# A two-layer decoder trunk on one core: the MLP groups' two matmuls with the high weights joined into one of 512 columns

## Chip, cores and metric

The kernel runs on one core of one Trainium2 chip. The metric is the device time of one execution in microseconds, as a median over runs. TensorE (PE) multiplies, VectorE (DVE) and ScalarE (ACT) do the elementwise work, and SyncE (SP) issues the large loads.

## What is computed

One sequence of 256 tokens of width 2048 passes through two layers. Layer 0 mixes tokens with a sparse attention (NSA), layer 1 with a differential attention. After each mixer stands an MLP of width 8192 with a squared ReLU. Vectors worked out from `c` scale, shift and gate every sub-layer. Cut to what matters here:

```python
for i in range(DEPTH):
    sh1, sc1, g1, sh2, sc2, g2 = jnp.split(mod_all[i][:, None, :], 6, axis=-1)
    ...
    x = x + g1 * y
    h = rms_norm(x, mlp_norm_g[i]) * (1.0 + sc2) + sh2
    x = x + g2 * (jnp.square(jax.nn.relu(h @ mlp_w1[i])) @ mlp_w2[i])
```

All inputs are float32.

## The kernel before

Each large product keeps float32 accuracy with numbers of the type `fp32r`. A weight tile `raw` (128x1024 float32, 512 KB) is loaded; ACT makes its rounded high part `wH`, and DVE the rest `wL = raw - wH` (`split`, L95 and L98 are the lines of the helpers `act` and `tt` through which most ACT and DVE work goes, L101 that of `stt`). Activations are kept in two parts as well: `at[:, 0]` is the high part, `at[:, 1]` the low one, each 128x256 per tile of 128 features. A product is the sum of three matmuls in PSUM: `wH` with the high activations, `wH` with the low ones, `wL` with the high ones (`ws_mm`, L239 to L241). The weights are the stationary operand there, so each matmul has 256 columns, the tokens. In `xs_mm` (L231 to L233) the roles are exchanged and each matmul has 512 columns of weights.

A **group** is 512 output features by 2048 inputs: 8 **units**, one `raw` tile each, and in a unit 8 blocks of 128 inputs by 128 outputs (`n` counts the four output blocks, `j` the two input blocks). The order in a unit is j outer, n inner; in the last unit it is n outer, so that the output blocks end one after another. A group `ws_group` has two PSUM banks with two output blocks in each, from a pool of four (`mm`); four further banks are the pools `sc` (three) and `sd` (one).

`mlp` (L552) runs, for each of four chunks `c` of 2048 hidden features, four groups of the first product (in the order below their tiles are named `m1_layer_c_nb_`; the profile calls them all `m`) and four groups of the second (`m2_layer_c_nb_`). The first two m1 groups of chunk 0 go through `pair`, which works on four banks per group. The other 30 groups of a layer are `ws_group`. After an m1 group ACT takes the ReLU out of PSUM (`rl`), squares it (`sq`) and rounds it into `hd`, and DVE makes the low part of `hd`. After an m2 group DVE adds the result, times a gate, to the residual `xT` (`residual`, one operation per output block).

Beside this run the reductions that give the modulation vectors: `ada_step` loads 512 KB tiles `adaraw`, and DVE multiplies and sums each. In layer 0's MLP there are 0.8 pairs of them per two units; all of them end before layer 1's MLP.

The program is written in this order, but a scheduler at build time sets the order of each engine's rows. Every engine then works strictly through its own rows: a row that waits holds up all behind it. `wH` and `wL` have three buffers each, `raw` five.

Of the kernel before, what the change touches and what calls it, by code (L numbers as in the profile page):

```python
# [19 lines left out]
P = 128  # L20
T = 256
# [54 lines left out]
def emit(ctx, tc, nc, a):  # L76
# [17 lines left out]
    def act(out, in_, func=AF.Copy, **kw):  # L94
        return S.activation(out=out, in_=in_, func=func, **kw)  # L95
# [4 lines left out]
    def stt(out, in0, scalar, in1, op0, op1, **kw):  # L100
        V.scalar_tensor_tensor(out, in0, scalar, in1, op0=op0, op1=op1, **kw)  # L101
# [7 lines left out]
    def sd(name):  # L109
        return sdp.tile([P, 512], F32, tag="sd", name=name)  # L110

    def sc(name):
        return scp.tile([P, 512], F32, tag="sc", name=name)
# [105 lines left out]
    def load(src, n=1024):  # L219
        raw = rawp.tile([P, 1024], F32, tag="raw", name="raw")  # L220
        last_load[0] = nc.sync.dma_start(raw[:, :n], src).ins
        return raw
# [12 lines left out]
    def ws_mm(ps, tiles, kt, H, L, off, first, last, w=T, m=P):  # L235
# [4 lines left out]
        TE.matmul(ps, H[:, off:off + m], xl, start=False, stop=False)  # L240
        TE.matmul(ps, L[:, off:off + m], xh, start=False, stop=last)  # L241

    def mm_tile(name):
        return mmp.tile([P, 512], F32, tag="mm", name=name)

# [14 lines left out]
    def ws_part(ps, srcs, tiles, rate, us, extra=None):  # L260
        for u in us:
            for hf in range(2):
                H, L = split(load(srcs(u)[hf]))
                for n, j in [(n, j) for n in range(4) for j in range(2)] if u * 2 + hf == 7 else \
                        [(n, j) for j in range(2) for n in range(4)]:
                        kt = u * 4 + hf * 2 + j
                        ws_mm(ps[n // 2][:, (n % 2) * T:(n % 2 + 1) * T], tiles, kt, H, L,
                              j * 512 + n * P, kt == 0 and n % 2 == 0, kt == KT - 1 and n % 2 == 1)
            ada_step(rate)
            if extra is not None:  # L270
                extra(u)

    def ws_group(name, srcs, tiles, rate):
        ps = [mm_tile(f"{name}{t}") for t in range(2)]
        ws_part(ps, srcs, tiles, rate, range(4))
        return ps

    def rstd_of(ps, t):
# [167 lines left out]
    class Turn:  # L446
# [20 lines left out]
        def pair(self, names, srcs, evac):  # L467
            l, w = self.l, self.which
            hh = None
            done = 0  # L470
            for g in range(2):
                if g == 0:
                    ps = [sc(f"{names[g]}{n}") for n in range(3)] + [mm_tile(f"{names[g]}3")]
                    pa = ps
                else:
                    ps = [mm_tile(f"{names[g]}{n}") for n in range(3)] + [sd(f"{names[g]}3")]
                for u in range(4):
                    for hf in range(2):
                        H, L = split(load(srcs[g](u)[hf]))
                        for j in range(2):  # L480
                            kt = u * 4 + hf * 2 + j
                            for n in range(4):
                                ws_mm(ps[n][:, :TW], self.z, kt, H, L, j * 512 + n * P,
                                      kt == 0, kt == KT - 1, TW)
                    p = g * 4 + u
                    if p == ZR:
                        self.r = self.st.rstd()
                        hh = [act_tile(f"hn_{l}_{w}_{i}") for i in range(4)]
                    if p >= ZR:
                        upto = -(-KT * (p - ZR + 1) // (8 - ZR))  # L490
                        for kt in range(done, upto):
                            modulate(hh, kt, self.r, Amod[:, l, w, kt:kt + 1],
                                     mod[:, l, 3 if w else 0, kt:kt + 1])
                        done = upto
                    if p == ZE:
                        evac(0, pa)
            evac(1, ps)
            return hh

    def residual(tn, ps, nb, l, vec, stats):  # L500
        for n in range(4):
            kt = nb * 4 + n
            stt(xT[:, kt, :], ps[n // 2][:, (n % 2) * T:(n % 2 + 1) * T], mod[:, l, vec, kt:kt + 1],
                xT[:, kt, :], ALU.mult, ALU.add)
            if stats:
                if nb == 3:
                    tn.scale(kt)
                tn.st.add(kt)
        if stats and nb == 2:
            tn.ready()  # L510
            for kt in range(12):
                tn.scale(kt)
# [39 lines left out]
    def mlp(l, tn, rates, final):  # L552
        for c in range(4):
            hid = [None] * 4 if c == 0 else [act_tile(f"hd_{l}_{c}_{i}") for i in range(4)]
            for nb in range(4):
                if c == 0 and nb < 2:
                    if nb == 1:
                        continue

                    def evac(g, zs):  # L560
                        hid[g] = act_tile(f"hd_{l}_0_{g}")
                        for b in range(2):
                            rl = sm.tile([P, 512], F32, tag="qr", bufs=QRB, name="rl")
                            for n in range(2):
                                z_evac(tn, zs, b * 2 + n, rl[:, n * T:(n + 1) * T], AF.Relu)
                            hidden(hid[g], b, rl)

                    h2 = tn.pair([f"m1_{l}_z{g}_" for g in range(2)],
                                 [lambda u, g=g: a["w1"][l, g, u] for g in range(2)], evac)
                    hid[2:] = [act_tile(f"hd_{l}_0_{g}") for g in range(2, 4)]  # L570
                    continue
                ps = ws_group(f"m1_{l}_{c}_{nb}_", lambda u: a["w1"][l, c * 4 + nb, u], h2, rates[1][nb] if c == 0 else rates[0])
                for b in range(2):
                    rl = sm.tile([P, 512], F32, tag="qr", bufs=QRB, name="rl")
                    act(rl, ps[b], AF.Relu)
                    hidden(hid[nb], b, rl)
            last = c == 3 and not final
            if last:
                tn = Turn(l + 1, 0)
            for nb in range(4):  # L580
                ps = ws_group(f"m2_{l}_{c}_{nb}_", lambda u: a["w2"][l, c, nb, u], hid, rates[1][4] if c == 0 and nb == 0 else rates[0])
                if c == 0 and nb == 0:
                    ada_until(l, 5)
                residual(tn, ps, nb, l, 5, last)
                if c == 3 and final:
                    for k0, k1 in ((0, 4),) if nb < 3 else ((0, 2), (2, 3), (3, 4)):
                        lo, hi = nb * 4 + k0, nb * 4 + k1
                        nc.sync.dma_start(a["out"][:, lo:hi, :], xT[:, lo:hi, :])
        return tn
# [451 lines left out]
```

## Time and profile before

| | us |
|---|---|
| median of 3 runs (2392.0 to 2394.16) | 2393.99 |
| the profiled execution | 2395.7 |
| its span | 2393.7 |
| PE busy | 2352.3 |
| DVE busy | 1688.2 |
| ACT busy | 1150.2 |

The span runs from the first to the last instruction of the program, and 2.0 us of the profiled execution lie around it. An engine's busy time is the union of its instructions. Consecutive matmuls overlap in the records, so what one of them costs is read from the distance between starts.

### The profile page before, as it was taken

Reading aid. Unit: us, or ns where it says so; the run is one execution under the profiler, and the core shown is the slowest. Engines: PE = TensorE matmul, PEld = TensorE weight load, DVE = VectorE, ACT = ScalarE, POOL = GpSimd, SP = SyncE. Lnnn points to the kernel's source line nnn. Section 1 sums busy time; section 2 is a strip of 40 time slices with the busy share of each in tenths; the row PEclk is TensorE's granted clock in tenths of the full one; section 3 lists DMA queues with packets and bytes.
Section 4 is the critical chain, followed back from the end, with each engine's and each line's share of the span. In section 5 each row is a group of like instructions: output and inputs, shape, how many; then the busy total and the mean of one; then the engine's idle time right before and its main releaser. Section 6 shows DMA issues by size and latency. Waiting matters only on the chain.

```text
span 2393.7 us, 42873 instructions
## 1 busy us (share of the span) xinstructions
PE 2352.3 (98%) x17171; PEld 2189.6 (91%) x17171; DVE 1688.2 (71%) x2594; ACT 1150.2 (48%) x1914; POOL 41.2 (2%) x41
## 2 busy tenths in 40 slices
PE   8998999989999999999999999999999999999999
PEld 5566778989999999999998778799999999999999
DVE  6776999899888887887887765666745445445454
ACT  2133577556435435435456555664643543543443
POOL 0001000000000000000000000100000000000000
PEclk9999999999999999999999999999999999999999
DMA  9988877888898998989986655445555555555554
GB/s 376 414 327 302 300 261 262 284 305 313 328 340 337 339 332 322 341 330 333 328 295 205 208 198 176 156 152 185 180 188 184 180 189 185 184 186 184 185 194 149
DMA packets 168887, 612.71 MB, mean 256 GB/s; under 512 B 18416, under 2 KB 19824, under 8 KB 168688
## 3 DMA queue, kind: packets, MB, share of 16 engines
q1 hardware_dynamic: 167536, 609.06, 72.2%
q8 instruction: 134, 2.20, 0.4%
q10 hardware_dynamic: 1152, 0.92, 0.1%
q14 instruction: 65, 0.53, 0.1%
HBM read 607.81 MB, written 2.10 MB: 255 GB/s over the span
## 4 chain that ended last, share of the span: by engine, by line
PE 86%; DVE 6%; DMA 4%; ACT 2%; issue 1%; POOL 1%; SPq 0%; DVEq 0%; ACTq 0%; POOLq 0%
PE m L241 19%; PE m L239 19%; PE m L240 19%; DMA adaraw<-adaT 2%; DMA adarow<-adaT 2%; DVE wL L98 2%; PE dwo L240 1%; PE dwo L239 1%; PE dwo L241 1%; PE psc L618 1%; DVE adaraw L101 1%; PE m_z L241 1%; PE m_z L240 1%; PE m_z L239 1%; DVE adarow L101 1%
## 5 line engine op out<-in xcount | busy, mean ns | idle before, releaser
L98 DVE TENSOR_TENSOR wL<-raw,wH 128x1024 fp32r<-128x1024 f32 x721 | 880.1, 1223 | 544.8 <-ACT wH L95 541.3
L95 ACT ACTIVATE wH<-raw 128x1024 fp32r<-128x1024 f32 x721 | 762.7, 1059 | 947.5 <-PE m L240 684.7
L240 PE MATMUL m<-hd,wH 128*128 128x256 f32 x2048 | 576.4, 281 | 0.0
L241 PE MATMUL m<-hd,wL 128*128 128x256 f32 x2048 | 576.3, 281 | 0.0
L239 PE MATMUL m<-hd,wH 128*128 128x256 f32 x2048 | 575.9, 281 | 0.0
L239 PE MATMUL m<-hn,wH 128*128 128x256 f32 x1792 | 504.4, 281 | 0.0
L241 PE MATMUL m<-hn,wL 128*128 128x256 f32 x1792 | 504.3, 281 | 0.0
L240 PE MATMUL m<-hn,wH 128*128 128x256 f32 x1792 | 504.1, 281 | 0.0
L101 DVE SCALAR_TENSOR_TENSOR adaraw<-adaraw,cbc 128x1024 f32<-128x1024 f32 x320 | 385.7, 1218 | 16.2 <-DMA adaraw<-adaT 15.9
L241 PEld LDWEIGHTS m<-hd,wL 128*128 128x128 f32 x2048 | 387.2, 189 | 0.0
L240 PEld LDWEIGHTS m<-hd,wH 128*128 128x128 f32 x2048 | 386.5, 189 | 0.0
L239 PEld LDWEIGHTS m<-hd,wH 128*128 128x128 f32 x2048 | 386.4, 189 | 0.0
L241 PEld LDWEIGHTS m<-hn,wL 128*128 128x128 f32 x1792 | 338.6, 189 | 0.0
L240 PEld LDWEIGHTS m<-hn,wH 128*128 128x128 f32 x1792 | 338.6, 189 | 0.0
L239 PEld LDWEIGHTS m<-hn,wH 128*128 128x128 f32 x1792 | 337.9, 189 | 0.2 <-ACT zb L95 0.2
L101 DVE SCALAR_TENSOR_TENSOR adarow<-adarow,cbc 128x2048 f32<-128x2048 f32 x32 | 73.2, 2287 | 14.1 <-DMA adarow<-adaT 14.1
L241 PE MATMUL m_z<-z,wL 128*128 128x258 f32 x256 | 70.9, 285 | 5.7 <-DVE wL L98 5.7
L241 PE MATMUL nwo<-o,wL 128*128 128x256 f32 x256 | 73.1, 286 | 1.5 <-DVE wL L98 1.5
L618 PEld LDWEIGHTS psc<-h,raw 128*128 128x128 f32 x256 | 49.5, 197 | 26.4 <-ACT h L95 17.9
L239 PE MATMUL nwo<-o,wH 128*128 128x256 f32 x256 | 73.3, 286 | 0.0
L239 PE MATMUL m_z<-z,wH 128*128 128x258 f32 x256 | 72.9, 286 | 0.0
L239 PE MATMUL dwo<-od,wH 128*128 128x256 f32 x256 | 72.9, 285 | 0.0
(300 smaller groups left out, 3326.8 us busy)
## 6 DMA issues: line engine op xcount, KB each, us to landing
raw<-w SPq DMA_DIRECT2D x512, 512.0 KB, 4.4
adaraw<-adaT SPq DMA_DIRECT2D x320, 512.0 KB, 5.5
raw<-di SPq DMA_DIRECT2D x96, 512.0 KB, 3.9
adarow<-adaT SPq DMA_DIRECT2D x32, 1024.0 KB, 11.8
raw<-wi SPq DMA_DIRECT2D x48, 512.0 KB, 5.9
raw<-ws SPq DMA_DIRECT2D x32, 512.0 KB, 10.3
raw<-nwo SPq DMA_DIRECT2D x32, 512.0 KB, 4.9
raw<-dwo SPq DMA_DIRECT2D x32, 512.0 KB, 3.4
```

Source lines behind the costliest of these rows:

```text
L95: return S.activation(out=out, in_=in_, func=func, **kw)
L98: V.tensor_tensor(out=out, in0=in0, in1=in1, op=op)
L101: V.scalar_tensor_tensor(out, in0, scalar, in1, op0=op0, op1=op1, **kw)
L239: TE.matmul(ps, H[:, off:off + m], xh, start=first, stop=False)
L240: TE.matmul(ps, H[:, off:off + m], xl, start=False, stop=False)
L241: TE.matmul(ps, L[:, off:off + m], xh, start=False, stop=last)
L618: TE.matmul(ps_c[i][n // 2][:, (n % 2) * T:(n % 2 + 1) * T], wc[:, i * 512 + n * P:i * 512 + (n + 1) * P], full, start=f and n % 2 == 0, s ...
```

## The change

The 60 groups of the two MLPs that were `ws_group` become `wide_group`. In it each block takes two matmuls instead of three (`wide_mm`): `wH` with both activation parts side by side, 512 columns that fill one PSUM bank, and `wL` with the high part, 256 columns onto the first half of that bank. A group has four banks, one per output block, and `bank_side` gives groups in turn the banks `sc, sc, sc, mm` and `mm, mm, mm, sd`. The two halves of a bank are added when it is emptied: after an m1 group ACT copies the second half (`half`), DVE adds it to the first, and ACT takes the ReLU from there; after an m2 group DVE adds each half to `xT` by itself. `pair` takes its banks through the same helper, unchanged.

```diff
--- before.py
+++ after.py
@@ -240,6 +240,19 @@
         TE.matmul(ps, H[:, off:off + m], xl, start=False, stop=False)
         TE.matmul(ps, L[:, off:off + m], xh, start=False, stop=last)
 
+
+
+    def wide_mm(ps, tiles, kt, H, L, off, first, last):
+        at = tiles[kt // 4][:, :, kt % 4, :T]
+        big = lambda stop: TE.matmul(ps.rearrange("p (a t) -> p a t", a=2), H[:, off:off + P], at,
+                                     start=first, stop=stop)
+        if last:
+            TE.matmul(ps[:, :T], L[:, off:off + P], at[:, 0], start=False, stop=False)
+            big(True)
+        else:
+            big(False)
+            TE.matmul(ps[:, :T], L[:, off:off + P], at[:, 0], start=False, stop=False)
+
     def mm_tile(name):
         return mmp.tile([P, 512], F32, tag="mm", name=name)
 
@@ -273,6 +286,27 @@
     def ws_group(name, srcs, tiles, rate):
         ps = [mm_tile(f"{name}{t}") for t in range(2)]
         ws_part(ps, srcs, tiles, rate, range(4))
+        return ps
+
+
+    def bank_side(name, side):
+        if side == 0:
+            return [sc(f"{name}{n}") for n in range(3)] + [mm_tile(f"{name}3")]
+        return [mm_tile(f"{name}{n}") for n in range(3)] + [sd(f"{name}3")]
+
+    side = [0]
+
+    def wide_group(name, srcs, tiles, rate):
+        ps = bank_side(name, side[0])
+        side[0] ^= 1
+        for u in range(4):
+            for hf in range(2):
+                H, L = split(load(srcs(u)[hf]))
+                for n, j in [(n, j) for n in range(4) for j in range(2)] if u * 2 + hf == 7 else \
+                        [(n, j) for j in range(2) for n in range(4)]:
+                    kt = u * 4 + hf * 2 + j
+                    wide_mm(ps[n], tiles, kt, H, L, j * 512 + n * P, kt == 0, kt == KT - 1)
+            ada_step(rate)
         return ps
 
     def rstd_of(ps, t):
@@ -469,11 +503,9 @@
             hh = None
             done = 0
             for g in range(2):
+                ps = bank_side(names[g], g)
                 if g == 0:
-                    ps = [sc(f"{names[g]}{n}") for n in range(3)] + [mm_tile(f"{names[g]}3")]
                     pa = ps
-                else:
-                    ps = [mm_tile(f"{names[g]}{n}") for n in range(3)] + [sd(f"{names[g]}3")]
                 for u in range(4):
                     for hf in range(2):
                         H, L = split(load(srcs[g](u)[hf]))
@@ -497,11 +529,12 @@
             evac(1, ps)
             return hh
 
-    def residual(tn, ps, nb, l, vec, stats):
+    def residual(tn, ps, nb, l, vec, stats, wide=False):
         for n in range(4):
             kt = nb * 4 + n
-            stt(xT[:, kt, :], ps[n // 2][:, (n % 2) * T:(n % 2 + 1) * T], mod[:, l, vec, kt:kt + 1],
-                xT[:, kt, :], ALU.mult, ALU.add)
+            parts = [ps[n][:, :T], ps[n][:, T:]] if wide else [ps[n // 2][:, (n % 2) * T:(n % 2 + 1) * T]]
+            for part in parts:
+                stt(xT[:, kt, :], part, mod[:, l, vec, kt:kt + 1], xT[:, kt, :], ALU.mult, ALU.add)
             if stats:
                 if nb == 3:
                     tn.scale(kt)
@@ -569,19 +602,23 @@
                                  [lambda u, g=g: a["w1"][l, g, u] for g in range(2)], evac)
                     hid[2:] = [act_tile(f"hd_{l}_0_{g}") for g in range(2, 4)]
                     continue
-                ps = ws_group(f"m1_{l}_{c}_{nb}_", lambda u: a["w1"][l, c * 4 + nb, u], h2, rates[1][nb] if c == 0 else rates[0])
+                ps = wide_group(f"m1_{l}_{c}_{nb}_", lambda u: a["w1"][l, c * 4 + nb, u], h2, rates[1][nb] if c == 0 else rates[0])
                 for b in range(2):
                     rl = sm.tile([P, 512], F32, tag="qr", bufs=QRB, name="rl")
-                    act(rl, ps[b], AF.Relu)
+                    for n in range(2):
+                        half = sm.tile([P, T], F32, tag="nsq", name="half", bufs=4)
+                        act(half, ps[b * 2 + n][:, T:])
+                        tt(rl[:, n * T:(n + 1) * T], ps[b * 2 + n][:, :T], half, ALU.add)
+                    act(rl, rl, AF.Relu)
                     hidden(hid[nb], b, rl)
             last = c == 3 and not final
             if last:
                 tn = Turn(l + 1, 0)
             for nb in range(4):
-                ps = ws_group(f"m2_{l}_{c}_{nb}_", lambda u: a["w2"][l, c, nb, u], hid, rates[1][4] if c == 0 and nb == 0 else rates[0])
+                ps = wide_group(f"m2_{l}_{c}_{nb}_", lambda u: a["w2"][l, c, nb, u], hid, rates[1][4] if c == 0 and nb == 0 else rates[0])
                 if c == 0 and nb == 0:
                     ada_until(l, 5)
-                residual(tn, ps, nb, l, 5, last)
+                residual(tn, ps, nb, l, 5, last, True)
                 if c == 3 and final:
                     for k0, k1 in ((0, 4),) if nb < 3 else ((0, 2), (2, 3), (3, 4)):
                         lo, hi = nb * 4 + k0, nb * 4 + k1
```

The scheduler sets the rows anew, and three places in layer 0's MLP are shown. The names: `hd`, `sq`, `rl`, `xT` as above, `mod` a modulation vector, the number behind a name tells tiles apart.

DVE, at the end of group m2_0_1_1 and the start of m2_0_1_2, before (the three `wL` are those of the new group's first three units):

```order
L98 TENSOR_TENSOR mod_135<-adaacc_7241 128x16
L98 TENSOR_TENSOR mod_135<-mod_135,smallT_94 128x16
L101 SCALAR_TENSOR_TENSOR Amod_136<-mod_135,smallT_94 128x16
L98 TENSOR_TENSOR wL_8475<-raw_8472,wH_8474 128x1024
L101 SCALAR_TENSOR_TENSOR xT_99<-m2_0_1_1_0_8198,mod_135,xT_99 128x256 x2
L98 TENSOR_TENSOR wL_8505<-raw_8502,wH_8504 128x1024
L101 SCALAR_TENSOR_TENSOR xT_99<-m2_0_1_1_1_8199,mod_135,xT_99 128x256 x2
L98 TENSOR_TENSOR wL_8535<-raw_8532,wH_8534 128x1024
```

and now (the two `wL` are those of the new group's first two units):

```order
L101 SCALAR_TENSOR_TENSOR xT_99<-m2_0_1_1_0_7608,mod_135,xT_99 128x256
L98 TENSOR_TENSOR mod_135<-adaacc_6829 128x16
L101 SCALAR_TENSOR_TENSOR xT_99<-m2_0_1_1_1_7609,mod_135,xT_99 128x256
L98 TENSOR_TENSOR mod_135<-mod_135,smallT_94 128x16
L101 SCALAR_TENSOR_TENSOR xT_99<-m2_0_1_1_0_7608,mod_135,xT_99 128x256
L101 SCALAR_TENSOR_TENSOR xT_99<-m2_0_1_1_1_7609,mod_135,xT_99 128x256
L101 SCALAR_TENSOR_TENSOR xT_99<-m2_0_1_1_2_7610,mod_135,xT_99 128x256
L101 SCALAR_TENSOR_TENSOR xT_99<-m2_0_1_1_3_7611,mod_135,xT_99 128x256
L101 SCALAR_TENSOR_TENSOR xT_99<-m2_0_1_1_2_7610,mod_135,xT_99 128x256
L101 SCALAR_TENSOR_TENSOR xT_99<-m2_0_1_1_3_7611,mod_135,xT_99 128x256
L98 TENSOR_TENSOR wL_7829<-raw_7826,wH_7828 128x1024
L98 TENSOR_TENSOR wL_7851<-raw_7848,wH_7850 128x1024
```

The new group's first `wL` stood ahead of the `xT` rows of the old group and now stands behind all eight of them.

ACT, at the end of group m1_0_1_0, before (the first two `wH` are those of the next group's first two units):

```order
L95 ACTIVATE wH_7121<-raw_7119 128x1024
L95 ACTIVATE wH_7151<-raw_7149 128x1024
L95 ACTIVATE rl_7105<-m1_0_1_0_0_6837 128x512
L95 ACTIVATE sq_7107<-rl_7105 128x512
L95 ACTIVATE rl_7111<-m1_0_1_0_1_6838 128x512
L95 ACTIVATE hd_0_1_0_6833<-sq_7107 128x2x256
L95 ACTIVATE sq_7113<-rl_7111 128x512
L95 ACTIVATE wH_7181<-raw_7179 128x1024
L95 ACTIVATE hd_0_1_0_6833<-sq_7113 128x2x256
```

and now (the first `wH` is the old group's last, the second the new group's first):

```order
L95 ACTIVATE wH_6683<-raw_6681 128x1024
L95 ACTIVATE half_6712<-m1_0_1_0_0_6505 128x256
L95 ACTIVATE half_6715<-m1_0_1_0_1_6506 128x256
L95 ACTIVATE half_6724<-m1_0_1_0_2_6507 128x256
L95 ACTIVATE wH_6741<-raw_6739 128x1024
L95 ACTIVATE rl_6711<-rl_6711 128x512
L95 ACTIVATE half_6727<-m1_0_1_0_3_6508 128x256
L95 ACTIVATE sq_6719<-rl_6711 128x512
L95 ACTIVATE wH_6763<-raw_6761 128x1024
```

The next group's first `wH` stood ahead of the work that empties the banks and now stands behind three copies out of the old group's banks.

PE, at the start of group m2_0_1_2, before:

```order
L239 MATMUL m2_0_1_2_0_8470<-hd_0_1_0_6833,wH_8474 128x256
L240 MATMUL m2_0_1_2_0_8470<-hd_0_1_0_6833,wH_8474 128x256
L241 MATMUL m2_0_1_2_0_8470<-hd_0_1_0_6833,wL_8475 128x256
L239 MATMUL m2_0_1_2_0_8470<-hd_0_1_0_6833,wH_8474 128x256
L240 MATMUL m2_0_1_2_0_8470<-hd_0_1_0_6833,wH_8474 128x256
L241 MATMUL m2_0_1_2_0_8470<-hd_0_1_0_6833,wL_8475 128x256
```

and now (the first row is the old group's last):

```order
L247 MATMUL m2_0_1_1_3_7611<-hd_0_1_3_6504,wH_7786 128x512
L247 MATMUL m2_0_1_2_0_7822<-hd_0_1_0_6501,wH_7828 128x512
L247 MATMUL m2_0_1_2_1_7823<-hd_0_1_0_6501,wH_7828 128x512
L247 MATMUL m2_0_1_2_2_7824<-hd_0_1_0_6501,wH_7828 128x512
L247 MATMUL m2_0_1_2_3_7825<-hd_0_1_0_6501,wH_7828 128x512
L254 MATMUL m2_0_1_2_0_7822<-hd_0_1_0_6501,wL_7829 128x256
L254 MATMUL m2_0_1_2_1_7823<-hd_0_1_0_6501,wL_7829 128x256
L254 MATMUL m2_0_1_2_2_7824<-hd_0_1_0_6501,wL_7829 128x256
L254 MATMUL m2_0_1_2_3_7825<-hd_0_1_0_6501,wL_7829 128x256
```

The first matmul that needs the new group's `wL` was the third row and is now the fifth, behind four wide ones.

## Rows read from the trace of the kernel before

**Rows 1.** The page, parts 1 and 4: busy time; the chain's share by engine

```profile
PE 2352.3 (98%) x17171; PEld 2189.6 (91%) x17171; DVE 1688.2 (71%) x2594; ACT 1150.2 (48%) x1914; POOL 41.2 (2%) x41
...
PE 86%; DVE 6%; DMA 4%; ACT 2%; issue 1%; POOL 1%; SPq 0%; DVEq 0%; ACTq 0%; POOLq 0%
```

**Rows 2.** Groups of the whole span: names, xcount | busy us, mean ns | idle us before

```profile
L240 PE MATMUL m<-hd,wH 128*128 128x256 f32 x2048 | 576.4, 281 | 0.0
L98 DVE TENSOR_TENSOR wL<-raw,wH 128x1024 fp32r<-128x1024 f32 x720 | 879.1, 1223 | 544.8 <-ACT wH L95 541.3 <-PE m L240 0.7
L95 ACT ACTIVATE wH<-raw 128x1024 fp32r<-128x1024 f32 x720 | 761.8, 1059 | 947.5 <-PE m L240 684.7 <-PE dwo L240 32.1 <-DMA raw<-wi 30.9
L101 DVE SCALAR_TENSOR_TENSOR adaraw<-adaraw,cbc 128x1024 f32<-128x1024 f32 x320 | 385.7, 1218 | 16.2 <-DMA adaraw<-adaT 15.9
```

**Rows 3.** A stretch of each MLP, columns in the first line

```profile
core 0: us, PE busy (x) PEld busy (x) DVE busy (x) ACT busy (x) POOL busy (x), PEclk, DMA share, GB/s
850.00:950.00 100.00, 100.00 (x842) 100.00 (x841) 79.97 (x106) 44.21 (x48) 0.00 (x0) 1.00 0.91 338
2000.00:2100.00 100.00, 100.00 (x842) 100.00 (x842) 50.06 (x49) 46.99 (x54) 0.00 (x0) 1.00 0.57 185
```

**Rows 4.** Timeline of PE (start us, us): first and last of 57 MLP matmuls

```profile
1899.77 0.28 PE L241 MATMUL m<-hn,wL 128*128 128x256 f32 x1
...
1906.43 0.28 PE L240 MATMUL m<-hn,wH 128*128 128x256 f32 x1
```

**Rows 5.** Timeline of PE, group dk1: first and last of 22 matmuls of 512 columns

```profile
1421.71 0.39 PE L233 MATMUL dk<-wH,hn 128*128 128x512 f32 x1
...
1426.58 0.39 PE L233 MATMUL dk<-wH,hn 128*128 128x512 f32 x1
```

**Rows 6.** Timeline of PE, fp32 matmuls of the first stage, 512 and 256 columns

```profile
126.46 3.60 PE L622 MATMUL psv<-raw,h 128*128 128x512 f32 x8
129.89 3.63 PE L618 MATMUL psc<-h,raw 128*128 128x256 f32 x16
133.36 3.60 PE L622 MATMUL psv<-raw,h 128*128 128x512 f32 x8
```

**Rows 7.** Timeline of ACT and of DVE in layer 1 near a group's end

```profile
1999.07 1.06 ACT L95 ACTIVATE wH<-raw 128x1024 fp32r<-128x1024 f32 x1 [1.79 <-PE m L240]
...
2000.16 1.22 DVE L98 TENSOR_TENSOR wL<-raw,wH 128x1024 fp32r<-128x1024 f32 x1 [1.62 <-ACT wH L95]
2001.31 1.65 DVE L101 SCALAR_TENSOR_TENSOR xT<-m,mod,xT 128x256 f32<-128x256 f32 x4
```

**Rows 8.** Groups of ACT and DVE by shape: durations near the change

```profile
L95 ACT ACTIVATE sq<-rl 128x512 f32<-128x512 f32 x64 | 40.1, 626 | 1.0
L95 ACT ACTIVATE on<-dops 128x256 f32<-128x256 f32 x16 | 6.0, 380 | 2.1 <-PE dops L865 2.1
L101 DVE SCALAR_TENSOR_TENSOR xT<-m,mod,xT 128x256 f32<-128x256 f32 x128 | 53.8, 476 | 9.7 <-PE m L241 9.7
L98 DVE TENSOR_TENSOR zy<-m_z,nst 128x256 f32<-128x256 f32 x16 | 5.8, 417 | 0.0
```

**Rows 9.** Timeline of PE and two stretches: two waits early in layer 0's MLP

```profile
514.94 0.75 PE L241 MATMUL m_z<-z,wL 128*128 128x258 f32 x4 [2.45 <-DVE wL L98]
...
529.46 0.75 PE L241 MATMUL m_z<-z,wL 128*128 128x258 f32 x4 [2.74 <-DVE wL L98]
...
517.00:525.00 8.00, 8.00 (x68) 8.00 (x68) 7.70 (x14) 3.95 (x5) 0.00 (x0) 1.00 0.91 319
529.00:534.00 5.00, 4.54 (x25) 4.54 (x26) 4.98 (x10) 2.26 (x5) 0.00 (x0) 0.66 0.47 172
```

**Rows 10.** Timeline of the program's end on PE and DVE

```profile
2389.75 0.28 PE L241 MATMUL m<-hd,wL 128*128 128x256 f32 x1
...
2390.07 0.88 DVE L101 SCALAR_TENSOR_TENSOR xT<-m,mod,xT 128x256 f32<-128x256 f32 x2 [0.55 <-PE m L241]
```

**Rows 11.** The page, part 6: DMA issues, KB each, us to landing

```profile
raw<-w SPq DMA_DIRECT2D x512, 512.0 KB, 4.4
```

## The prediction

> **What bounds the kernel now.** I read busy time and the chain that ended last [rows 1]: PE is busy for 98% of the span and holds 86% of the chain. Then the stretches [rows 3]: in both MLPs PE is busy for 100.00 of 100 us at a granted clock of 1.00 (2.4 GHz), while DVE has 80 us in layer 0 and 50 in layer 1, ACT 44 and 47. So nothing is waited for in the MLPs but the matmuls themselves, and what counts is the distance between their starts. The reader should not take the 281 ns of the groups [rows 2] for it: those records overlap. In the timeline 57 matmuls of 256 columns start in 6.66 us, 56 distances, so 118.9 ns each [rows 4]. Where the weights move, 22 of 512 columns start in 4.87 us, 21 distances, so 231.9 ns [rows 5].
>
> **What the matmuls give.** A block had three of 256 columns, 3 x 118.9 = 356.7 ns. Now it has one of 512 and one of 256: 231.9 + 118.9 = 350.8. That is 5.9 ns less: the columns are the same, and only a fixed part of one matmul goes away. There are 60 groups x 64 blocks = 3840 blocks, so 22.7 us, half of it in each layer. No row has this wide matmul itself, with activations in two stretches as the moving operand. From above it is bounded by two narrow ones, 237.8 ns, where the gain is 0. From below I take an fp32 matmul of 256 columns, which moves slower per column: sixteen take 133.36 - 129.89 = 3.47 us, 217 ns each [rows 6], and a gain of 21 ns a block, 80 us. I take 231.9, the same columns of the same type into the same full bank. Each ns off is 3.8 us.
>
> By the Trainium skill, "TensorE: Matmul & The Clock Gate", section Back-to-back issue gap, a warm matmul of N columns takes N/2.4 + 2.5 ns, so the fixed part would be 2.5 ns and the gain 9.6 us. The trace differs for this type, 118.9 against 109.2 and 231.9 against 215.8, so the sum stays with the rows.
>
> **Work that is added.** After an m1 group ACT copies four halves (380 ns, as a copy of that size out of PSUM took) and DVE adds four (417, as `zy`); the ReLU, now out of SBUF, costs as much as `sq` [rows 8]. After an m2 group DVE has eight `xT` rows for four. Four of them run in 1.65 us, and with 476 ns for the last they start 0.39 apart [rows 7, 8]. In layer 0 that is some 1.6 us of DVE per group of 192 x 0.1189 = 22.8 us, or 7%: 80% becomes 87 and does not bind. Bytes are the same, and a DMA share of 0.91 rises by 1%. A `raw` tile that is freed 3 us late has five buffers to spare, 14 us, for 4.4 us of landing [rows 11]. Banks are reused after one whole group of some 22 us, so that no matmul waits for them. These cost nothing, under the cover of PE, as long as `wH` and `wL` come in time.
>
> **Where they don't.** A unit takes 8 x 0.351 = 2.81 us. ACT rounds a tile when PE frees the buffer of three units before, DVE follows, and `wL` is done 2.31 us after ACT began [rows 7], with two units, 5.6 us, until PE wants it. That slack of about 3.3 us covers whatever stands ahead of `wL` unless that waits for the end of the old group. In layer 1 the scheduler keeps the next group's first two `wL` ahead of all but the first `xT` row, which waits for the first bank alone, so I count nothing there. In layer 0 the scheduler put old work first in ten places.
>
> Let E be when the old group's last matmul has had its turn. In the last unit the banks end 0.70 us apart. At the program's end DVE starts 0.32 us after the start of the last matmul, whose record is 0.28 long [rows 10]; a wide record is 0.39 [rows 5], so bank 3 is seen at E - 0.23 + 0.43 = E + 0.20 and the others at -0.50, -1.20 and -1.90.
>
> End of m2_0_1_1, the first place shown in the order: the second `xT` row starts at -1.20, a `mod` row of 0.2 follows, and at 0.39 apart the eighth starts at about +1.3. `wL` runs from 1.7 to 2.94. PE first has four wide matmuls, 0.93 us, and then waits some 2.1. m2_0_2_3 is alike; m2_0_0_0 has no `mod` row, 1.9; m2_0_3_0 has two statistics rows too, 2.7. At the end of m2_0_3_2 sixteen rows stand ahead of the second unit's `wL`, which ends at about 6.1 where PE wants it at 2.81 + 0.93: 2.4. Sum 11.2 us.
>
> End of m1_0_1_0, the second place: the third copy starts at -0.50, `wH` follows at -0.17 and takes 1.06 [rows 2], so PE waits 0.94 for it. `wL` is done at 0.92 + 1.23 = 2.2, 0.3 after the four wide ones. Together 1.3, and the same behind m1_0_2_2. Behind m1_0_1_1 and m1_0_2_3 the third unit's `wH` is the eleventh row after a copy, and its `wL` comes behind two `adaraw` and two `hd` rows: by the same durations 1.1 each. Behind m1_0_1_2 0.8. Sum 5.6.
>
> So PE waits 16.8 us that it did not before. These could be some 12 if ACT and DVE overlap better than I lay them end to end, and 20 if a load comes late.
>
> Each wait can also cost clock. Before, one of 2.74 us was followed by a fall: 0.66 granted over 5 us, that is 1.7 us lost, partly at 1.2 GHz; after one of 2.45 us it stayed 1.00 [rows 9]. I count a fall after the two longest, 3.4 us, and bound it by 0 and by all ten, 17. The last bank at the program's end has two `xT` rows as before, but they depend on each other: 0.4 at most.
>
> **The sum.** 2395.7 (the profiled execution) - 22.7 + 16.8 + 3.4 + 0.4 = 2393.6. The median of the runs lies 1.7 below that execution, so 2392, or 0.1% less: no change that a measurement of this kernel can tell, which I put at 0.2%, 4.8 us.
>
> **The rivals.**
> *The waits hardly show* (5 us, no fall of the clock): 2394 - 22.7 + 5.4 = 2377. For it speaks that the scheduler had late work before too, and PE never waited in these groups [rows 3]; against it that then the first `wL` stood ahead of the rows that wait. Chance 0.20.
> *The wide matmul is no better than two narrow ones.* If the jump between the two activation stretches costs what a second matmul does, 237.8 ns, the gain is 0 and the waits stay: 2394 + 20.6 = 2415. From 235 on, where the gain is 11.5, the kernel is slower, 2403. No row shows fp32r operands in two stretches. Chance 0.20.
> By the rule of the skill cited above, the gain would be 9.6 us and the time 2405; this is counted with this rival.
> *A cheap wide matmul*, 217 ns: 2392 - 57 = 2335. Chance 0.04, as nothing of this type ran so fast.
> *Every wait lowers the clock*, from some 0.8 us on: 13.6 more, 2406. The 2.45 us without a fall speak against it. Chance 0.04.
>
> **How the numbers follow.** My case has 0.52, with a range of its own from 2383 to 2401 (2 ns of the wide matmul, 4 us of the waits); of it 0.40 lies within 0.2%, 0.09 under 2389.2 and 0.03 above 2398.8. With the rivals: faster 0.09 + 0.20 + 0.04 = 0.33, same 0.40, slower 0.03 + 0.20 + 0.04 = 0.27. The range of 2376 to 2406 leaves out the cheap matmul, about half of *the waits hardly show*, and the upper part of the second rival, 0.2 in all.
>
> **What would show it.** In the changed profile 512-column matmuls should stand 232 ns and 256-column ones 119 from the next start. An undisturbed group should take 22.45 us instead of 22.8, and layer 1's MLP end 11 us sooner after its start. PE should be idle for 1 to 3 us in ten places of layer 0, at the first unit after m2_0_0_0, m2_0_1_1, m2_0_2_3, m2_0_3_0, m1_0_1_0 and m1_0_2_2 and at the second or third after the other four, ended by DVE `wL` or ACT `wH`, and nowhere in layer 1. A wide distance of 235 or more, no such idle time, or a clock below 1.00 in more than two places would make the prediction wrong, each by the amount above.

## The result, and the profile after

The changed kernel takes 2407.33 us (median of 6 runs, 2405.65 to 2411.98) against 2394.07 of the old one beside it, a ratio of 1.0055 with an interval of 1.0045 to 1.0065: slower by 13 us. Forecast were 2392 us and a range that ended at 2406.

The profiled execution took 2410.28 us (span 2408.3), 14.6 more than that of before. Where they came from is read from the start of each stage's first matmul in both timelines. Before the first wide group, where both kernels issue the same instructions, the changed kernel is 4.2 us later (565.95 against 561.74). Layer 0's wide groups take 704.5 us from the start of their first matmul to that of the matmul behind their last, against 686.3: 18.2 more. The attention between gives back 0.7. Layer 1's wide groups, behind which no matmul comes, take 7.7 less to the start of their last. The end, behind the last matmul, is 0.6 longer (4.53 against 3.93). Sum: 4.2 + 18.2 - 0.7 - 7.7 + 0.6 = 14.6.

So one change did two things: it gained in layer 1 and lost in layer 0. The page of the changed kernel, parts 1 and 4, answering [rows 1]:

```profile
PE 2346.4 (97%) x13331; PEld 2002.0 (83%) x13331; DVE 1772.9 (74%) x2834; ACT 1178.7 (49%) x2026; POOL 43.2 (2%) x41
...
PE 82%; DVE 7%; DMA 5%; ACT 2%; issue 2%; POOL 1%; SPq 0%; DVEq 0%; ACTq 0%; POOLq 0%
```

PE has 6 us less work in a longer span, and its share of the chain fell from 86 to 82%, while DVE's rose from 6 to 7% and DMA's from 4 to 5%. The costliest groups (busy us, mean ns | idle us before), answering [rows 2]:

```profile
L98 DVE TENSOR_TENSOR wL<-raw,wH 128x1024 fp32r<-128x1024 f32 x721 | 877.9, 1222 | 445.3 <-ACT wH L95 442.4
...
L247 PE MATMUL m<-hd,wH 128*128 128x512 f32 x2048 | 709.1, 398 | 0.9 <-ACT wH L95 0.9
...
L254 PE MATMUL m<-hd,wL 128*128 128x256 f32 x1920 | 530.0, 282 | 10.3 <-DVE wL L98 10.1
...
L101 DVE SCALAR_TENSOR_TENSOR xT<-m,mod,xT 128x256 f32<-128x256 f32 x256 | 108.7, 478 | 37.7 <-PE m L247 37.6
```

The idle time before the second PE row is new: 10.3 us before matmuls that read `wL`, put down to DVE, where the old groups had 0.0:

```profile
L241 PE MATMUL m<-hd,wL 128*128 128x256 f32 x2048 | 576.3, 281 | 0.0
```

Stretches of the changed kernel, answering [rows 3], with one more that covers nearly all of layer 0's wide groups:

```profile
core 0: us, PE busy (x) PEld busy (x) DVE busy (x) ACT busy (x) POOL busy (x), PEclk, DMA share, GB/s
850.00:950.00 100.00, 100.00 (x569) 87.00 (x568) 85.27 (x120) 44.85 (x54) 0.00 (x0) 1.00 0.86 321
2000.00:2100.00 100.00, 100.00 (x569) 87.17 (x568) 55.63 (x65) 46.31 (x56) 0.00 (x0) 1.00 0.57 186
570.00:1235.00 665.00, 651.25 (x3652) 560.68 (x3651) 572.01 (x828) 309.95 (x393) 0.00 (x0) 1.00 0.87 325
```

The 100 us that the prediction looked at in layer 0 look as full as before: PE 100.00, DVE 85. Only the long stretch shows the loss, PE 651.25 of 665 us, and DVE there has 572 of 665, 86%, where 87 was forecast. The waits sit at group boundaries, and a window can miss all of them.

Layer 1 shows the gain alone. The first and the last matmul of its wide groups in PE's timeline (start us, us), changed kernel:

```profile
1726.87 0.40 PE L247 MATMUL m<-hn,wH 128*128 128x512 f32 x1
...
2403.74 0.39 PE L247 MATMUL m<-hd,wH 128*128 128x512 f32 x1
```

and the kernel before:

```profile
1705.15 0.28 PE L239 MATMUL m<-hn,wH 128*128 128x256 f32 x1
...
2389.75 0.28 PE L241 MATMUL m<-hd,wL 128*128 128x256 f32 x1
```

676.87 against 684.60 us, for the same 1920 blocks: 352.6 ns a block against 356.6, a gain of 4.0 ns where 5.9 had been forecast. Between starts, a wide matmul holds 234.6 ns on average (236.7 where a second wide one follows, in a group's last unit), and the narrow one 118.0. Forecast were 231.9 and 118.9.

Layer 0 shows what the prediction looked for. At the end of m2_0_1_1, DVE of the changed kernel:

```profile
842.49 0.48 DVE L101 SCALAR_TENSOR_TENSOR xT<-m,mod,xT 128x256 f32<-128x256 f32 x1
842.89 0.17 DVE L98 TENSOR_TENSOR mod<-mod,smallT 128x16 f32<-128x16 f32 x1
842.97 2.44 DVE L101 SCALAR_TENSOR_TENSOR xT<-m,mod,xT 128x256 f32<-128x256 f32 x6
845.33 3.49 DVE L98 TENSOR_TENSOR wL<-raw,wH 128x1024 fp32r<-128x1024 f32 x3
```

and PE:

```profile
843.18 1.33 PE L247 MATMUL m<-hd,wH 128*128 128x512 f32 x5
846.60 0.73 PE L254 MATMUL m<-hd,wL 128*128 128x256 f32 x4 [2.09 <-DVE wL L98]
```

Eight `xT` rows wait for the old group's banks one after the other, the next group's first `wL` comes behind them at 845.33, and PE starts the first matmul that needs it at 846.60. By the distance of starts PE lost 2.25 us; 2.1 had been worked out for this place. Some of the waits of layer 0's MLP, engine, line, releaser: us, times, longest us:

```profile
ACT wH L95 <- DMA raw<-w: 89.1, 51, 6.8
...
PEld m L254 <- DVE wL L98: 21.9, 20, 3.3
...
PEld m L247 <- ACT wH L95: 4.6, 7, 1.0
```

Weight loads of PE wait 21.9 us for `wL`, in 20 places, and 4.6 for `wH`; the kernel before had neither row in this stage. ACT's `wH` waits 89.1 us for `raw`, where it was 27.2 before:

```profile
ACT wH L95 <- DMA raw<-w: 27.2, 11, 3.5
```

Most of that is hidden. It is not hidden in five groups. For one of them, SP's queue at 1025 us shows what stood ahead of the late load:

```profile
1025.32 8.60 SPq L164 DMA_DIRECT2D adaraw<-adaT  x2
1034.01 1.47 SPq L221 DMA_DIRECT2D raw<-w  x2
1035.88 2.61 SPq L164 DMA_DIRECT2D adaraw<-adaT  x2
1038.58 1.36 SPq L221 DMA_DIRECT2D raw<-w  x3
```

Two `adaraw` loads hold the head of the queue for 8.6 us, the second until the DVE row that reads its buffer is done, and the `raw` loads behind them start late. DVE had waited 1.87 us for the old group's first bank, and this row came behind eight `xT` rows (seven are shown) and two `wL`:

```profile
1026.93 0.48 DVE L101 SCALAR_TENSOR_TENSOR xT<-m,mod,xT 128x256 f32<-128x256 f32 x1 [1.87 <-PE m L247]
...
1028.46 2.44 DVE L101 SCALAR_TENSOR_TENSOR xT<-m,mod,xT 128x256 f32<-128x256 f32 x6
...
1032.34 1.22 DVE L101 SCALAR_TENSOR_TENSOR adaraw<-adaraw,cbc 128x1024 f32<-128x1024 f32 x1
```

ACT, whose last column names what it waited for:

```profile
1039.67 1.06 ACT L95 ACTIVATE wH<-raw 128x1024 fp32r<-128x1024 f32 x1 [6.84 <-DMA raw<-w]
```

PE, which needs this `wH` in the fifth unit of m2_0_2_2, then waits 0.58 us. Some 9 to 14 us ahead of each of the other four waits the trace has the same pattern: DVE's `adaraw` row runs behind rows that empty the old group's banks (at 706.30, 822.65, 1055.18 and 1149.00 us), and SP issues the next `adaraw` load only when it ends. But this does not make PE wait by itself. In layer 0's MLP such loads waited 382.3 us for DVE (131 times, 7.8 at most), and before the change already 359.0 us (126 times, 7.6 at most), with no wait of PE.

Last, the clock after four of the waits, in stretches of 10 us (last three columns: granted clock, DMA share, GB/s):

```profile
844.00:854.00 10.00, 7.91 (x46) 6.61 (x45) 9.75 (x15) 3.07 (x3) 0.00 (x0) 1.00 0.88 327
1077.00:1087.00 10.00, 7.91 (x38) 6.84 (x38) 8.20 (x12) 2.63 (x3) 0.00 (x0) 0.83 0.88 326
1194.50:1204.50 10.00, 7.26 (x42) 5.99 (x40) 9.72 (x15) 6.07 (x11) 0.00 (x0) 1.00 0.77 286
1246.00:1256.00 10.00, 7.18 (x27) 6.28 (x28) 8.20 (x12) 2.79 (x5) 0.00 (x0) 0.66 0.72 234
```

It fell behind the wait of 2.26 us (1076.68) and in the course of that of 3.02 (1245.57), and not with those of 2.25 (844.12) and 2.90 (1194.52).

### The profile page after: what moved, and what is told of

Its sections match the earlier page's. It is cut to its first block, busy times and chain, and to the rows that moved or that the text cites. A ratio compares the mean times of both kernels' runs of the same rounds, so it can differ in the third digit from the quotient of the medians.

```text
span 2408.3 us, 35573 instructions
## 1 busy us (share of the span) xinstructions
PE 2346.4 (97%) x13331; PEld 2002.0 (83%) x13331; DVE 1772.9 (74%) x2834; ACT 1178.7 (49%) x2026; POOL 43.2 (2%) x41
## 4 chain that ended last, share of the span: by engine, by line
PE 82%; DVE 7%; DMA 5%; ACT 2%; issue 2%; POOL 1%; SPq 0%; DVEq 0%; ACTq 0%; POOLq 0%
PE m L247 34%; PE m L254 17%; DVE wL L98 2%; DMA adaraw<-adaT 2%; DMA raw<-w 1%; DVE adaraw L101 1%; PE psc L655 1%; PE dwo L240 1%; PE dwo L239 1%; PE dwo L241 1%; PE psv L659 1%; DMA adarow<-adaT 1%; PE m_z L241 1%; PE m_z L240 1%; PE m_z L239 1%
## 5 line engine op out<-in xcount | busy, mean ns | idle before, releaser
L247 PE MATMUL m<-hd,wH 128*128 128x512 f32 x2048 | 709.1, 398 | 0.9 <-ACT wH L95 0.9
L247 PE MATMUL m<-hn,wH 128*128 128x512 f32 x1792 | 622.9, 398 | 1.4 <-ACT wH L95 1.4
L254 PE MATMUL m<-hd,wL 128*128 128x256 f32 x1920 | 530.0, 282 | 10.3 <-DVE wL L98 10.1
L247 PEld LDWEIGHTS m<-hd,wH 128*128 128x128 f32 x2048 | 377.0, 189 | 81.1 <-ACT wH L95 1.9
L247 PEld LDWEIGHTS m<-hn,wH 128*128 128x128 f32 x1792 | 329.8, 189 | 71.4 <-ACT wH L95 2.7
L101 DVE SCALAR_TENSOR_TENSOR xT<-m,mod,xT 128x256 f32<-128x256 f32 x256 | 108.7, 478 | 37.7 <-PE m L247 37.6
L239 PE MATMUL nwo<-o,wH 128*128 128x256 f32 x256 | 73.4, 287 | 0.0
L239 PE MATMUL dwo<-od,wH 128*128 128x256 f32 x256 | 73.0, 285 | 0.0
L239 PE MATMUL m_z<-z,wH 128*128 128x258 f32 x256 | 73.0, 287 | 0.0
L240 PE MATMUL m_z<-z,wH 128*128 128x258 f32 x256 | 72.8, 286 | 0.0
L240 PE MATMUL nwo<-o,wH 128*128 128x256 f32 x256 | 72.7, 284 | 0.0
L240 PE MATMUL dwo<-od,wH 128*128 128x256 f32 x256 | 72.3, 282 | 0.0
L241 PE MATMUL dwo<-od,wL 128*128 128x256 f32 x256 | 72.2, 282 | 0.0
```

Source lines behind the costliest of these rows:

```text
L239: TE.matmul(ps, H[:, off:off + m], xh, start=first, stop=False)
L247: big = lambda stop: TE.matmul(ps.rearrange("p (a t) -> p a t", a=2), H[:, off:off + P], at, start=first, stop=stop)
L254: TE.matmul(ps[:, :T], L[:, off:off + P], at[:, 0], start=False, stop=False)
```

## The experiments

Three theories stood against each other. **ORDER**: the matmul gains some 16 us, and in layer 0 more than that is lost because old evacuation rows stand ahead of the next group's first weights. **WORK**: the added copies, adds and `xT` rows cost time wherever they stand. **STRETCHES**: the matmul over two activation stretches is what disappoints. Diffs are against the changed kernel. The spans of the MLPs below are those of a layer's wide groups, taken as above: in layer 0 to the start of the next matmul, in layer 1 to that of the last.

**e1_late_evac: the same rows, issued later.**

```diff
...
+                if later and u * 2 + hf >= 1:
+                    with tc.issue_after(rows[0]), tc.issue_after(rows[1]):
+                        later.pop(0)()
...
-                    hidden(hid[nb], b, rl)
+                    hidden(dst, b, rl)
+                later.extend(lambda b=b, f=evac_b: f(b) for b in range(2))
...
+                    later.extend(lambda f=f: f() for f in residual_parts(tn, ps, nb, l, 5, last))
...
```

> The changed kernel, but each MLP group's evacuation is held back: its rows are issued behind the next group's second wH on ACT and second wL on DVE (two pieces, behind units 1 and 2). Matmuls, banks, copies and adds are the same in number and form. Theory ORDER (the changed kernel loses only because in layer 0 old evacuation rows stand ahead of the next group's first weights; those waits and the two clock falls hold 23 + 4 us, and the matmul itself gives 16.7): 2394 - 16.7 + 0.6 at the end = 2378 us, to 2381 if late loads stay; PE idle nowhere over 0.5 us at the starts of layer 0's MLP groups. Theory WORK (the added copies, adds and the longer hold on PSUM cost time wherever they stand): 2400 to 2410 us, with the waits moved to the second or third unit. Theory STRETCHES (the matmul over two activation stretches is what disappoints): the order matters little, 2400 or more.

Measured 2387.01 us (10 runs), a ratio of 0.9969 [0.9960, 0.9978]: faster than both kernels, though not by the 16 us hoped for. Layer 0's wide groups take 683.85 us instead of 704.5, and layer 1's 676.87 as in the changed kernel. Waits of layer 0's MLP:

```profile
ACT wH L95 <- DMA raw<-w: 132.2, 76, 5.8
...
PEld m L257 <- DVE wL L98: 5.4, 6, 2.4
...
PE m L257 <- DVE wL L98: 3.0, 2, 2.0
```

All ten places are gone. ACT waits for `raw` even longer than in the changed kernel, 132 us, and PE loses 0.2 us to it in m2_0_1_1, 0.4 in m2_0_2_3 and perhaps a part of a wait in m2_0_3_2. Why late loads cost 3.3 us in the changed kernel and less here stays open: none of the five groups that they held up there begins with one of the ten waits. Two longer waits are left, 1.20 us in m2_0_3_2 and 2.15 in m2_0_3_3, both behind a group's start, and a fall of the clock behind the second. The second wait is of the edit's own making: the twelve scale rows were handed over in two pieces of six. DVE:

```profile
1229.37 2.47 DVE L101 SCALAR_TENSOR_TENSOR z<-xT,Amod,z 128x256 fp32r<-128x256 f32 x6
1231.75 1.22 DVE L98 TENSOR_TENSOR wL<-raw,wH 128x1024 fp32r<-128x1024 f32 x1
```

Six `z` rows stand ahead of the fifth unit's `wL`, which PE then waits for. Without these 6.2 us (all waits, their restarts and the fall) layer 0 would have 677.6, as the changed kernel would without its own (677.4). WORK falls: the same rows, later, cost nothing that shows.

**e2_three_narrow: new banks and evacuation, old matmuls.**

```diff
-        big = lambda stop: TE.matmul(ps.rearrange("p (a t) -> p a t", a=2), H[:, off:off + P], at,
-                                     start=first, stop=stop)
+
+        def big(stop):
+            TE.matmul(ps[:, :T], H[:, off:off + P], at[:, 0], start=first, stop=False)
+            TE.matmul(ps[:, T:], H[:, off:off + P], at[:, 1], start=False, stop=stop)
```

> The changed kernel with the one wide matmul written as two of 256 columns into the two halves of the same bank: new banks, new evacuation, old matmuls. The scheduler then puts the next group's first wH and wL ahead of the old rows almost everywhere in layer 0. ORDER: 2394 to 2398 us, the old pitch of 118.9 ns and hardly a wait, so the added evacuation work costs next to nothing by itself. WORK: the loss of the changed kernel (13 us) and the 16.7 us that the matmul gave there come on top of 2394: about 2424 us. STRETCHES: about 2394 us, as the wide matmul is gone.

Measured 2396.82 us, 1.0010 [1.0001, 1.0020]. Layer 0's groups take 687.2 us, layer 1's 685.2: 0.8 and 0.6 more than before. That is the most that the new evacuation costs by itself; PE waits over 0.15 us only once, and those 0.62 us, in m2_0_0_3, are most of layer 0's 0.8. The scheduler's order depends on the matmuls: with three narrow ones it put the first weights ahead of most of the old rows, with the wide one behind them.

**e3_one_stretch: the same order, another layout.**

```diff
...
+    def flat_tile(name):
+        return actp.tile([P, 4, 2, T], F32R, tag="act", name=name).rearrange("p k a t -> p a k t")
...
-                        hh = [act_tile(f"hn_{l}_{w}_{i}") for i in range(4)]
+                        hh = [flat_tile(f"hn_{l}_{w}_{i}") for i in range(4)]
...
-            hid = [None] * 4 if c == 0 else [act_tile(f"hd_{l}_{c}_{i}") for i in range(4)]
+            hid = [None] * 4 if c == 0 else [flat_tile(f"hd_{l}_{c}_{i}") for i in range(4)]
...
```

> The changed kernel with the MLP's activation tiles laid out so that the high and low part of one 128-row block lie side by side (512 columns in one stretch); the instructions and their order are the same. STRETCHES: the distance behind a wide matmul falls from 234.6 to 231.9 ns, 3840 x 2.7 = 10 us: 2397 us. ORDER: the waits are all still there; if the layout does not matter for the distance, 2407 us, and 234.6 is the cost of going between the wide and the narrow form in one bank.

Measured 2399.45 us, 1.0024 [1.0015, 1.0034]. The first and last wide-group matmul of layer 1:

```profile
1717.67 0.40 PE L250 MATMUL m<-hn,wH 128*128 128x512 f32 x1
...
2392.26 0.40 PE L250 MATMUL m<-hd,wH 128*128 128x512 f32 x1
```

Its 674.59 us are 351.4 ns a block, and 2.3 us less than with two stretches. In layer 0, blocks without a wait fell from 352.9 ns (234.7 for the wide matmul, 118.2 for the narrow one) to 350.6 (232.4 and 118.1), 4.4 us. So the second stretch cost 6.7 us in all, two thirds of what STRETCHES said; on average a wide matmul over one stretch holds 232.4 to 232.9 ns where 231.9 had been forecast. The ten waits are all still there (1.91 us behind m2_0_0_0, 2.34 behind m2_0_1_1), as ORDER said. Of the 7.9 us between this median and the changed kernel's the remaining 1.2 are within what the front of the program varies (below).

**e4_layer1_only: the change in layer 1 alone.**

```diff
+WIDE = (1,)
...
-                    for n in range(2):
+                    for n in range(2 if l in WIDE else 0):
...
-                    act(rl, rl, AF.Relu)
+                    act(rl, rl if l in WIDE else ps[b], AF.Relu)
...
-                residual(tn, ps, nb, l, 5, last, True)
+                residual(tn, ps, nb, l, 5, last, l in WIDE)
```

> The change in layer 1 alone; layer 0's MLP has the old groups, banks and evacuation. ORDER: layer 1 has no waits, so it keeps its 7.7 us: 2394 - 7.7 + 0.6 = 2387 us. WORK: layer 1 pays half of the loss too: 2397 to 2401 us. STRETCHES: by the distances in the changed kernel also about 2387, so this run tells ORDER from WORK alone.

The groups are chosen in the same way (`wide_group if l in WIDE else ws_group`). Measured 2391.63 us, 0.9985 [0.9975, 0.9995]: faster than before, by 3 us where 7 were expected. In its profile layer 0's groups take 686.34 us and layer 1's 676.87, ORDER's numbers, and the execution took 2388.3, 7.4 less than that of before. Its ten runs lie between 2387.4 and 2395.2, so the profiled one was among the quickest; where the others spend 3 us more, no profile shows.

**e6_layer1_old_first: the bad order where there is room.** (e5 follows below.)

```diff
-        tt(L[:, :n], raw[:, :n], H[:, :n].bitcast(F32), ALU.subtract)
+        if hold[1]:
+            hold[1] -= 1
+            with tc.issue_after(hold[0]):
+                tt(L[:, :n], raw[:, :n], H[:, :n].bitcast(F32), ALU.subtract)
...
+                hold[1] = 2 if l == 1 and not (c == 3 and nb == 3) else 0
```

> The changed kernel, and in layer 1, which has no waits, the first two wL behind each m2 group (15 places) are held behind all eight old xT rows, the order that the scheduler chose in layer 0. ORDER: each place makes PE wait some 1.9 to 2.1 us: 15 x 2.0 = 30 us in layer 1's MLP, 677 becomes 707, and 2407 becomes 2437 us, more if the clock falls. If layer 0's waits come from its load on DMA and DVE and not from the order, layer 1 has the room to hide this and stays at 677 us, 2407 in all.

Measured 2446.84 us, 1.0223 [1.0207, 1.0240]. Layer 1's groups take 714.1 us instead of 676.9. DVE at one of the fifteen places:

```profile
2005.71 3.07 DVE L101 SCALAR_TENSOR_TENSOR xT<-m,mod,xT 128x256 f32<-128x256 f32 x7
2008.70 3.48 DVE L98 TENSOR_TENSOR wL<-raw,wH 128x1024 fp32r<-128x1024 f32 x3
```

and PE:

```profile
2006.88 1.32 PE L254 MATMUL m<-hd,wH 128*128 128x512 f32 x5
2009.97 0.76 PE L261 MATMUL m<-hd,wL 128*128 128x256 f32 x4 [1.77 <-DVE wL L98]
```

From 2006.88 five wide matmuls, the old group's last and the next one's first four, last until 2009.97, 3.09 us instead of 5 x 0.232 = 1.16: 1.93 lost, and each of the fifteen places lost between 1.92 and 1.93. That is 28.9 us, as forecast to within 0.1 us a place. The order alone makes the wait, in a layer where DMA has a share of 0.57 and DVE 56 of 100 us. The other 8 us are 2.5 of late restarts and small delays and 5.9 of clock, in four falls. Four stretches of 10 us behind four of these waits, each 1.93 us long:

```profile
1792.00:1802.00 10.00, 8.23 (x47) 6.85 (x46) 7.44 (x10) 3.18 (x3) 0.00 (x0) 1.00 0.55 190
1842.00:1852.00 10.00, 8.23 (x39) 6.82 (x38) 5.88 (x8) 2.64 (x3) 0.00 (x0) 0.83 0.61 204
1868.00:1878.00 10.00, 8.24 (x48) 6.88 (x47) 6.94 (x8) 2.83 (x3) 0.00 (x0) 1.00 0.59 206
2057.00:2067.00 10.00, 8.24 (x39) 6.76 (x38) 5.89 (x8) 2.72 (x3) 0.00 (x0) 0.83 0.62 209
```

The clock falls after the second and the fourth and stays after the first and the third. Nothing in the waits themselves tells them apart.

**e5_late_one_stretch, and once more as e8: both remedies.** The edits of e1 and e3 together, with the scale rows in four pieces and the last group's rows inside the next pair (cut; the first two lines are against e1):

```diff
...
-            out += [lambda: scales(0, 6), lambda: scales(6, 12)]
+            out += [lambda k=k: scales(k, k + 3) for k in range(0, 12, 3)]
...
+                        if later and g == 0 and u * 2 + hf >= 1:
+                            with tc.issue_after(rows[0]), tc.issue_after(rows[1]):
+                                later.pop(0)()
...
```

> Late evacuation and one stretch together; the twelve scale rows of the last groups of layer 0 are spread over four units, and the last group's evacuation stands behind the second unit of the group pair that follows. ORDER with STRETCHES as a size: layer 1's MLP takes 674.6 us as in the run with one stretch (10.0 less than the old kernel), layer 0's 686.3 - 11.3 + 1.2 for the wait in m2_0_3_2 that stays = 676; with 0.6 at the end 2394.75 - 10.0 - 10.1 + 0.6 = 2375 us. If the two do not add up, because the waits come back elsewhere in layer 0 (a DMA share over 0.9 leaves little), 2380 to 2387.

Measured 2383.07 us (5 runs), 0.9946 [0.9933, 0.9959]. The MLPs have what was expected, 676.6 and 674.6 us; the whole was 8 us longer than expected, 5.4 of them before the first wide group. So it was run again.

> Late evacuation with one stretch, once more. Its MLPs had the time that was expected (676.6 and 674.6), yet the run was 8 us longer than expected, 5.4 of them before the first wide group and 1 in layer 1's attention. If that is chance, the MLPs take 676 to 677 and 674 to 675 again while the first wide group starts at 559 to 563, and the median falls to 2375 to 2380; if it belongs to the kernel (tiles at other places in SBUF), the start is at 567 again and the median 2383.

Measured 2379.94 us, 0.9932 [0.9920, 0.9945], MLPs 675.2 and 674.6, the first wide group at 564.22. At the end of m2_0_1_1 DVE now has:

```profile
832.62 2.50 DVE L98 TENSOR_TENSOR wL<-raw,wH 128x1024 fp32r<-128x1024 f32 x2 [0.72 <-ACT wH L95]
835.04 1.66 DVE L101 SCALAR_TENSOR_TENSOR xT<-m,mod,xT 128x256 f32<-128x256 f32 x4
836.61 1.22 DVE L98 TENSOR_TENSOR wL<-raw,wH 128x1024 fp32r<-128x1024 f32 x1
837.75 1.66 DVE L101 SCALAR_TENSOR_TENSOR xT<-m,mod,xT 128x256 f32<-128x256 f32 x4
```

Both first `wL` come ahead of all old rows, at 832.62, and the third between the two halves; PE loses nothing there. In its two runs this kernel is 12 and 17 us faster than the kernel before. The MLPs give 19.7 and 21.1 against before. Most of what is missing lies before the first wide group, at 567.14 and 564.22 against 561.74. The second start fits neither guess, 559 to 563 for chance and 567 for the kernel; as both lie inside the range of the other profiles (below), nothing speaks for the tiles' new places in SBUF.

**e7_change_again: which part recurs.** No edit.

> The changed kernel as it is, once more, to see which part of its time recurs. ORDER: layer 0's wide MLP groups take 704 us again, within 3 for the falls of the clock, and layer 1's 677, for they hang on the order of the instructions. The 4.2 us that its profiled execution had lost before the first wide group (561.74 against 565.95) lie where both kernels issue the same instructions: if they are chance, this start moves between 559 and 567 as in the other profiles, and the median stays within 2402 to 2410; if they belong to the change, it stands at 566 again.

Measured 2408.20 us, 1.0040 [1.0025, 1.0056]. Layer 0's groups take 702.2 us and layer 1's 676.87. The ten waits came again, nine of them within 0.03 us of the first time and the tenth at 2.73 for 3.02. The late loads cost some 3.9 us instead of 3.3 and lie partly in other groups (1.49 us in m2_0_2_2, where 0.58 had been), and the clock fell once among layer 0's wide groups instead of twice. This profiled execution was the slowest of its four runs (2414.0): the first wide group started at 569.76, later than in any other profile. In the nine others, which issue the same instructions up to there, it lies between 559.75 and 567.14. So the start of the wide groups varies by 10 us among kernels that are alike up to there, and the 4.2 us of the first profile are no effect of the change that could be shown. It can't be ruled out either: of the ten starts the changed kernel's own two are the latest and the third latest, and 569.76 fits neither of the two expectations.

## Why the prediction was wrong

**Right.** The mechanism, its places and, to 0.6 us each, its sizes. All ten places waited, and nowhere in layer 1:

| wait behind | m2_0_0_0 | m2_0_1_1 | m2_0_2_3 | m2_0_3_0 | m2_0_3_2 | m1_0_1_0 | m1_0_2_2 | m1_0_1_1 | m1_0_2_3 | m1_0_1_2 |
|---|---|---|---|---|---|---|---|---|---|---|
| forecast us | 1.9 | 2.1 | 2.1 | 2.7 | 2.4 | 1.3 | 1.3 | 1.1 | 1.1 | 0.8 |
| measured us | 1.88 | 2.25 | 2.26 | 2.90 | 3.02 | 1.10 | 1.10 | 0.87 | 0.86 | 0.55 |

Both rows add up to 16.8, by luck: the five m2 places waited 1.1 us longer than forecast, the five m1 places 1.1 less. That the added work is hidden held too: e2 puts it at 1.4 us at most in both layers, and in e1 the same rows cost nothing that shows when they come after the weights. The rival *the waits hardly show* fell here, and *every wait lowers the clock* with two falls for ten waits.

**Wrong, the first step: "I take 231.9, the same columns of the same type into the same full bank."** The matmul that moves two stretches held 234.6 ns. The layers gained 16.7 us (7.7, and 8.9 in layer 0 once waits and clock are taken off) instead of 22.7: 6.0 us. With one stretch the step would have held in sum: e3 and e8 give 10.0 in layer 1, and e8 686.3 - 675.2 + 2.1 of waits = 13.2 in layer 0, 23.2 together. The rows of dk1 had their moving columns side by side, and the prediction carried their price over to an operand that has not; its own rival (237.8 ns) had the right direction and went twice too far. (That rival's gain at 235 ns, 11.5 us, is a slip: 2.8 ns on 3840 blocks are 10.8, and its time there 2404.) By the rule of the Trainium skill, "TensorE: Matmul & The Clock Gate", Back-to-back issue gap, which the page gives for an isolated matmul, the gain would have been 9.6 us and the time 2405. The time came out near that by luck: no gain measured here, 16.7 or 23.2, agrees with it.

**Wrong, the second step: "These cost nothing, under the cover of PE, as long as `wH` and `wL` come in time", and with it "A `raw` tile that is freed 3 us late has five buffers to spare".** The buffers were counted, the queue was not. The rows held back on DVE were also what frees `adaraw` buffers; their loads stood at the head of SP's queue and `raw` loads behind them. With this PE waited 3.3 us more in five groups, and some 3.9 in e7. That the queue is the cause is read from the trace and not shown: no run changed the queue alone, and holds as long cost PE nothing in the kernel before. A further 2.7 us are small, most of them because the matmul behind one that waited comes 0.1 us late. Waits were thus 22.8 us, not 16.8: 6.0 us. The sum had 20 as its upper bound "if a load comes late".

**Near, by luck: "I count a fall after the two longest", 3.4 us.** Two falls cost 4.3 us. But they came with the longest and after one of 2.26, not after the second longest, and in e7 there was one, after a wait of 2.26.

With 0.2 more at the end and 3.5 outside the wide groups (4.2 - 0.7), which no run ties to the change, this is 6.0 + 6.0 + 0.9 + 0.2 + 3.5 = 16.6, from the 2393.6 of the sum to 2410.3 of the profiled execution. The median lies 3.0 below that execution, where 1.7 were counted.

**Which theory stands.** ORDER, shown from both sides: e1 moves the rows and the waits go, e6 moves them in layer 1 and the waits come, at the forecast size. WORK falls by e1 and e2. STRETCHES holds as a part, 6.7 us, which covers the 6.0 of the first wrong step. The second wrong step has no run of its own, and its cause stays open.

## What to carry to other kernels

A change that makes the bound engine's work shorter can make a scheduler set everything around it in another order: read the order at each group boundary and ask whether the next group's first operands stand behind rows that wait for the old group's end. If they do, tie the old rows behind the second unit's operands; here this turned a loss of 13 us into a gain of 7 to 8, and with the layout of 12 to 17. When a row is held, also follow its buffers to the queue that waits for them, and count what is queued behind.

## What was not expected of the hardware

A moving operand of 2 x 256 columns in two stretches held TensorE 234.6 ns on average (layer 1), and 236.7 ahead of another such; the same columns side by side (e3) held it 232.9 and 228.9. The matmul behind one that had waited came 0.1 us late, some twenty times in layer 0. And of fifteen waits of 1.92 to 1.93 us in the same place of a group (e6) four were followed by a granted clock of 0.83 over 10 us, that is partly 1.2 GHz, and the other eleven by 1.00.
